# RWKV-7 and RetNet layer on one core: triangular blocks solved from the last row, the result transposed once

## The chip, the core and the metric

The kernel runs on one core of a Trainium2 chip. The engines of the core work side by side: TensorE (PE in the rows, its weight loads PEld) multiplies matrices, VectorE (DVE) works element by element, ScalarE (ACT) evaluates functions and copies, GpSimd (POOL) does a little of both, SyncE (SP) issues most of the DMAs. The metric is the device time of one execution in microseconds, as the median of several runs.

## What is computed

One decoder layer: 256 tokens, width 2048, float32. Half of the mixing width is RWKV-7 with 16 heads of 64, half is RetNet with 4 heads of 256; then an output projection, a norm, an MLP and a second norm.

```python
def _wkv7_scan(r, decay, k, v, a_vec, b_vec):
    def step(S, inp):
        r_t, w_t, k_t, v_t, a_t, b_t = inp
        sa = jnp.einsum('bhvk,bhk->bhv', S, a_t)
        S = (S * w_t[:, :, None, :] + sa[..., None] * b_t[:, :, None, :]
             + v_t[..., None] * k_t[:, :, None, :])
        y_t = jnp.einsum('bhvk,bhk->bhv', S, r_t)
        return S, y_t
...
def _hybrid_layer(x, ...):
    h = x @ w_in
    y_a = _rwkv7_mix(h[..., :RWKV_SHIFT_WIDTH], ...)
    q, k, v, g = jnp.split(h[..., RWKV_SHIFT_WIDTH:], RET_SPLITS, axis=-1)
    y_b = _retention_mix(q, k, v, g, ret_gn_w)
    mix = jnp.concatenate([y_a, y_b], axis=-1).astype(x.dtype) @ w_o
    x = _layer_norm(ALPHA * x + mix, ln1_w, ln1_b)
    ff = jnp.square(jax.nn.relu(x @ w_up)) @ w_down
    return _layer_norm(ALPHA * x + ff, ln2_w, ln2_b)
```

The recurrence over tokens is computed in chunks of 64. Within a chunk, what the state gains from earlier tokens of the same chunk is a triangular system: the inverse of a 64x64 triangular matrix for every head and chunk. That inverse is what the change touches.

## The kernel before

**Projections.** Every weight tile comes by DMA (`raw`, three buffers, L135), ScalarE casts it to a short float `whi` (L136), VectorE takes the rest `wlo` (L138), and TensorE multiplies three times for each product: `whi` with the high part of x, `whi` with the low part, `wlo` with the high part. `stat_tile` (L154) holds the weights and streams x through, 256 columns; `mov_chunk` (L170) does it the other way round, 512 columns. A weight tile has two halves, and a half is 24 matmuls of L154 or 12 of L170.

**Units.** The first 512 us hold four units u = 0 to 3 of four RWKV heads each (`rwkv_unit`), and retention's four heads between them. `large()` writes out the projections; `interleave` lets the units' generators take a step every so many projection steps (`LAG`). A unit waits in the text for a key of another with `until(...)`. The order of each engine's instructions is not the order of the text, though: a scheduler of the framework places them as its model holds them ready, so a small edit can move work far from it.

**One unit.** Decay: `s` (L542), a running sum `cs` over the 256 tokens of both head pairs as one scan of 512 elements (L544; the constant at `C_RS` is zero at the start of each chunk, which restarts the sum), exponentials `dc`, `di`, `s` on ScalarE (L548 to L550). Keys: `kkr` (L571), the square `sq`, and a head sum, that is `hi` on ScalarE (L558), `lo` on VectorE (L559) and two matmuls with a matrix of ones (L562, L563). The same head sum serves the bonus `bo` later in the unit. Then the Gram products `g1` (L623) and their mask (L625).

**The triangular blocks.** Each 64x64 triangle of `g1` is split in 32x32 blocks. The two on the diagonal are inverted by VectorE, the one off it by two matrix products `d1` (L726) and `d2` (L737). There are 16 triangles in a unit. `g1` goes to DRAM (`dn`), and from there into `blk`: 128 partitions, in four groups of 32, and each partition holds one block of 32x32 elements, row s behind row s − 1, every block four times with fewer rows each time (`diag`, L641). `xb` holds eight columns of the inverse for each partition and starts as pieces of the unit matrix (`eye`). The loop at L674 goes t = 1 to 31. Step t multiplies what is known of m = min(t, 8) pieces, t elements each, with column t of `blk` (`prod`, L677) and sums each piece into `xb` (L680). With t growing, fewer groups are at work: q = 128 partitions down to 32. The result goes by four DMAs to DRAM (`dxt`, L687) and by two into `xt` (L689). VectorE then turns the upper halves of it into `xx` (L715, two 32x256 transposes), `d1` multiplies `g1` with `xx`, ScalarE copies the product to `pt`, `d2` multiplies `pt` with `xt`, a copy puts that into `xt` (L742), and the scans of the chunks (L758 to L792) follow.

**Retention.** For each head VectorE multiplies q and k with the rotary table, `ra` (L417) and `rb` (L419), POOL turns them into `qk` (L422, L423), TensorE multiplies q with k (L434), VectorE multiplies with the mask `dmt` into `pm` (L439). `dmt` is loaded on POOL's queue.

**SBUF.** `LONG` names tiles with a buffer of their own; other names of `tmp` share `NSHORT` = 10 buffers.

Of the kernel before, what the change touches and what calls it, by code (L numbers as in the profile page):

```python
# [10 lines left out]
F32 = mybir.dt.float32  # L11
# [3 lines left out]
ALU = mybir.AluOpType  # L15
AX = mybir.AxisListType

P = 128
# [19 lines left out]
C_BO = C_RS + 512  # L38
# [3 lines left out]
def constants():  # L42
# [10 lines left out]
    rs = np.ones(512, np.float32)  # L53
    rs[::64] = 0.0
    c[:, C_RS:C_RS + 512] = rs
# [11 lines left out]
    eye = np.tile(np.eye(8, 32, dtype=np.float32).reshape(1, 256), (P, 1))  # L67
# [33 lines left out]
def tile_hybrid_layer(ctx, tc, xT, xtok, ws, pp, lup, glup, ln1r, ln2r, cst, rope, dmask, eye, out):  # L101
# [169 lines left out]
    with ExitStack() as rctx:  # L271
# [3 lines left out]
        LONG = ("k", "r", "v", "ar", "g1", "g2", "btok", "ktok", "vtok", "xt", "gg", "bg", "yc")  # L275
# [3 lines left out]
        def tmp(name, bufs=1, n=512):  # L279
            if name in LONG or n < 256:  # L280
                return rp.tile([P, n], F32, name=name, tag=name, bufs=2 if name in TWO else bufs)
            if name in RET:
                return rp.tile([P, n], F32, name=name, tag="rshort", bufs=4)
            return rp.tile([P, n], F32, name=name, tag="short", bufs=NSHORT)
# [11 lines left out]
        def diag(d, g, n):  # L296

            return bass.AP(tensor=d.tensor, offset=d.offset + 8 * 65 * g, ap=[[2080, 32], [64, n], [1, 32 - 8 * g]])
# [98 lines left out]
        def retention():  # L397

            for n in range(2):
# [9 lines left out]
                for h in (2 * n, 2 * n + 1):  # L409
# [21 lines left out]
                    dmt = rp.tile([P, T], F32, name="dmt", tag="dmt", bufs=2)  # L431
# [71 lines left out]
        def rwkv_unit(u):  # L503
# [4 lines left out]
            def until(*key):  # L508
                while key not in done:
                    yield 1  # L510
# [27 lines left out]
            for p, j in enumerate(js):  # L538
# [5 lines left out]
            V.tensor_tensor_scan(out=cs, data0=c1[:, C_RS:C_RS + 512], data1=s, initial=0.0,  # L544
                                 op0=ALU.mult, op1=ALU.add)
# [87 lines left out]

            g1v = g1.rearrange("q (g two x) -> q g two x", two=2, x=64)
# [4 lines left out]
            for g in range(4):  # L639
                m = 32 - 8 * g  # L640
                nc.sync.dma_start(out=blkv[32 * g:32 * g + 32, 0:m, 0:m], in_=diag(dn, g, m))  # L641
# [32 lines left out]
            for t in range(1, 32):  # L674
                q, m = 32 * ((39 - t) // 8), min(t, 8)
                pv = prod[0:q, 0:m * t].rearrange("q (j s) -> q j s", s=t)
                V.tensor_tensor(out=pv, in0=xbv[0:q, 0:m, 0:t],  # L677
                                in1=blk.rearrange("q (s t) -> q t s", t=32)[0:q, t:t + 1, 0:t].broadcast_to([q, m, t]),
                                op=ALU.mult)
                V.tensor_reduce(out=xbv[0:q, 0:m, t], in_=pv, axis=AX.X, op=ALU.add)  # L680
                if t in SUB_YIELD:
                    yield LAG["sub"]
            if u > 0:
                yield from until("end", u - 1)
            xt = tmp("xt")
            for g in range(4):
                nc.sync.dma_start(out=diag(dxt, g, 8), in_=xbv[32 * g:32 * g + 32, :, 0:32 - 8 * g])  # L687
            for h in range(2):
                nc.sync.dma_start(out=v8(xt)[64 * h:64 * h + 64], in_=rows(dxt, h))  # L689
# [5 lines left out]
            yield from until("v", u)  # L695
            v = done["v", u]
# [15 lines left out]
            xx = tmp("xx")[:, 0:256]  # L712
            for h in range(2):
                q = slice(64 * h, 64 * h + 32)
                V.transpose(out=xx[q].rearrange("q (g x) -> q g x", x=32), in_=v8(xt)[q, :, 0:32])  # L715
# [8 lines left out]
            def d1(r, p, n):  # L724
                o = 128 * (4 * p + n)
                TE.matmul(pb[r.start + 32:r.stop, c32(p, n)], g1[r.start:r.start + 32, o + 32:o + 64],  # L726
                          xx[r.start:r.start + 32, c32(p, n)], start=True, stop=True)
# [426 lines left out]
```

## Time and profile before

| what | value |
| --- | --- |
| median of 3 runs | 1284.11 us (1282.04 to 1285.03) |
| the profiled execution | 1282.36 us |
| its span | 1280.6 us |
| mean granted clock of TensorE | 0.991 |
| TensorE busy | 1233.7 us, 96% of the span |
| VectorE busy | 853.1 us, 67% |
| ScalarE busy | 560.0 us, 44% |
| GpSimd busy | 117.3 us, 9% |

The profiled execution lies among the runs; the rows below are of it, and its times are counted from the start of its span. The shares are averages over stages of a different kind: the units and retention up to about 512 us, then the output projection and the MLP.

### The profile page before, as it was taken

The numbers are of one execution on the slowest core, as the hardware profiler recorded it, in microseconds if no ns is written. First come the engines' busy times: TensorE is split into PE (matmuls) and PEld (weight loads), VectorE is DVE, ScalarE is ACT, GpSimd is POOL, SyncE is SP. The second block draws the span as 40 slices with busy tenths as digits, with TensorE's granted clock in tenths as the row PEclk, the third lists the DMA queues.
The fourth block names the chain that finished last, engine by engine and source line by source line (L and its number), as shares of the span: only waits on it lengthen the run. The fifth ranks groups of instructions, "written<-read, shape, count | busy, mean of one in ns | idle before, by whom it ended". The sixth has DMA issues, their size and how long they took to land.

```text
span 1280.6 us, 21924 instructions
## 1 busy us (share of the span) xinstructions
PE 1233.7 (96%) x8952; PEld 1110.1 (87%) x8952; DVE 853.1 (67%) x1311; ACT 560.0 (44%) x723; POOL 117.3 (9%) x97
## 2 busy tenths in 40 slices
PE   7998989999998999989999999999999999999996
PEld 7988888878897778769988899988999888999885
DVE  6898899899979765685654455545555554555566
ACT  5544335355434343464443344433444433444441
POOL 1100121110102100137300000000000000000001
PEclk9999999999999999999999999999999999999998
DMA  8565345345454437555655555555555555555562
GB/s 287 197 187 157 105 142 168 108 153 176 156 144 148 147 112 252 197 176 193 239 198 198 194 188 190 184 192 190 194 190 190 184 192 192 193 190 186 183 213 98
DMA packets 86185, 229.89 MB, mean 180 GB/s; under 512 B 30530, under 2 KB 30658, under 8 KB 85316
## 3 DMA queue, kind: packets, MB, share of 16 engines
q1 hardware_dynamic: 83924, 219.51, 52.5%
q0 software_dynamic: 1440, 7.87, 1.7%
q8 instruction: 70, 1.15, 0.4%
q10 hardware_dynamic: 720, 1.11, 0.3%
q14 instruction: 31, 0.25, 0.1%
HBM read 224.72 MB, written 3.74 MB: 178 GB/s over the span
## 4 chain that ended last, share of the span: by engine, by line
PE 75%; DVE 11%; ACT 3%; DMA 3%; issue 2%; POOL 1%; DVEq 0%; ACTq 0%; POOLq 0%; SPq 0%
PE mm L170 33%; PE mm L154 33%; PE mm L190 4%; DVE wlo L138 3%; DMA raw<-in_ws_dram 2%; DVE prod L677 2%; DVE xb L680 1%; PE sm L623 1%; ACT whi L136 1%; DMA xt<-dxt 1%; POOL qk L423 1%; ACT wx L136 0%; PE sm L766 0%; ACT sw L653 0%; PE sm L758 0%
## 5 line engine op out<-in xcount | busy, mean ns | idle before, releaser
L138 DVE TENSOR_TENSOR wlo<-raw,whi 128x1024 fp32r<-128x1024 f32 x375 | 466.6, 1245 | 330.4 <-ACT whi L136 319.6
L136 ACT CAST whi<-raw 128x1024 fp32r<-128x1024 f32 x376 | 395.0, 1051 | 548.5 <-PE mm L154 235.3
L154 PE MATMUL mm<-x1h,wlo 128*128 128x256 f32 x960 | 269.9, 281 | 0.0
L154 PE MATMUL mm<-x1l,whi 128*128 128x256 f32 x960 | 269.9, 281 | 0.0
L154 PE MATMUL mm<-x1h,whi 128*128 128x256 f32 x960 | 269.8, 281 | 0.0
L154 PEld LDWEIGHTS mm<-x1h,wlo 128*128 128x128 f32 x960 | 183.6, 191 | 0.0
L154 PE MATMUL mm<-xh,whi 128*128 128x256 f32 x640 | 181.8, 284 | 0.0
L154 PEld LDWEIGHTS mm<-x1h,whi 128*128 128x128 f32 x960 | 181.1, 189 | 0.1
L154 PEld LDWEIGHTS mm<-x1l,whi 128*128 128x128 f32 x960 | 180.2, 188 | 0.2
L154 PE MATMUL mm<-xl,whi 128*128 128x256 f32 x640 | 179.9, 281 | 0.0
L154 PE MATMUL mm<-xh,wlo 128*128 128x256 f32 x640 | 179.8, 281 | 0.0
L170 PE MATMUL mm<-whi,ul 128*128 128x512 f32 x448 | 174.3, 389 | 0.0
L170 PE MATMUL mm<-whi,uh 128*128 128x512 f32 x448 | 174.3, 389 | 0.0
L170 PE MATMUL mm<-wlo,uh 128*128 128x512 f32 x448 | 174.3, 389 | 0.0
L154 PEld LDWEIGHTS mm<-xh,whi 128*128 128x128 f32 x640 | 121.5, 190 | 2.9 <-issue 0.9
L154 PEld LDWEIGHTS mm<-xl,whi 128*128 128x128 f32 x640 | 121.5, 190 | 0.9 <-issue 0.2
L154 PEld LDWEIGHTS mm<-xh,wlo 128*128 128x128 f32 x640 | 121.6, 190 | 0.7
L170 PEld LDWEIGHTS mm<-whi,ul 128*128 128x128 f32 x448 | 84.1, 188 | 17.5
L170 PEld LDWEIGHTS mm<-whi,uh 128*128 128x128 f32 x448 | 84.1, 188 | 17.5
L170 PEld LDWEIGHTS mm<-wlo,uh 128*128 128x128 f32 x448 | 84.1, 188 | 17.1
L1044 POOL TENSOR_TENSOR z<-z,lnr 128x512 f32<-128x512 f32 x3 | 3.9, 1292 | 603.0 <-DVE stats L1032 603.0
L170 PE MATMUL mm<-whi,xh 128*128 128x512 f32 x128 | 51.7, 404 | 0.0
(270 smaller groups left out, 1612.5 us busy)
## 6 DMA issues: line engine op xcount, KB each, us to landing
raw<-in_ws_dram SPq DMA_DIRECT2D x400, 512.0 KB, 4.5
first<-in_ws_dram SPq DMA_DIRECT2D x8, 256.0 KB, 8.2
z<-in_xtok_dram POOLq DMA_DIRECT2D x2, 1024.0 KB, 10.8
lnr<-in_ln1r_dram POOLq DMA_DIRECT2D x2, 1024.0 KB, 5.5
lnr<-in_ln2r_dram POOLq DMA_DIRECT2D x2, 1024.0 KB, 11.2
xraw<-in_xT_dram SPq DMA_DIRECT2D x3, 512.0 KB, 8.8
dn<-g SPq DMA_DIRECT2D x8, 128.0 KB, 3.6
xt<-dxt SPq DMA_DIRECT2D x8, 128.0 KB, 3.6
```

The lines of the kernel that those rows point to most:

```text
L136: S.copy(hi, raw)
L138: E.tensor_tensor(out=lo, in0=raw, in1=hi.bitcast(F32), op=ALU.subtract)
L154: TE.matmul(dst, w[:, c], a, start=n == 0, stop=n == 3 * KT - 1)
L170: TE.matmul(dsts[tt], a, w[:, c], start=first and k4 == 0 and j == 0, stop=last and k4 == 3 and j == 2)
L190: TE.matmul(dst, a, wt[:, o:o + w], start=kq == 0 and k4 == 0 and i == 0, stop=kq == 3 and k4 == 3 and i == 2)
L423: G.tensor_tensor(out=o[:, hs[1]], in0=rb_[:, hs[0]], in1=rb_[:, hs[1]], op=ALU.add)
L623: TE.matmul(bank[r, 128 * n:128 * n + 128], src[r, c64(p, n)], ar[r, o:o + 128], start=True, stop=True)
L677: V.tensor_tensor(out=pv, in0=xbv[0:q, 0:m, 0:t], in1=blk.rearrange("q (s t) -> q t s", t=32)[0:q, t:t + 1, 0:t].broadcast_to([q, m, t]), ...
L680: V.tensor_reduce(out=xbv[0:q, 0:m, t], in_=pv, axis=AX.X, op=ALU.add)
L1044: G.tensor_tensor(out=z[:, tt, cb(n)], in0=z[:, tt, cb(n)], in1=lnr2[:, 0, cb(n)], op=ALU.mult)
```

## The change

The loop runs the same triangle from its last row. Step t takes s0 = 31 − t and multiplies the t known elements behind s0 with row s0 of `blk`, from s0 + 1 on. Where before the elements of that operand were 32 elements (128 bytes) apart, they now lie one behind the other. The pieces sit at the end of their rows, not at the start: `blk` is filled from 32 − m on, `xb` and `eye` are shifted by 24 or 8 − m places, and `diag` reads from another offset; the DMAs' shapes stay. What comes out is the inverse transposed, `xc`, a new tile with its own buffer. `d1` reads `xc` itself, so `xx` is gone; `xt` is made from `xc` by one 128x512 transpose before `d2`. The wait for the end of the unit before (`until("end", u - 1)`) stands behind the DMAs now, since `xc` and no longer `xt` is what they fill.

Room for `xc` comes from two places. `dmt` has one buffer, not two. The constant at `C_RS` has 256 columns, not 512, so its DMA is 128x640 and no longer 128x896, and the scan is two scans of 256.

```diff
--- before.py
+++ after.py
@@ -35,7 +35,7 @@
 C_ID = 0
 C_MG = 128
 C_RS = 256
-C_BO = C_RS + 512
+C_BO = C_RS + 256
 NC1 = C_BO + 128
 
 
@@ -50,9 +50,9 @@
         c[r, C_MG:C_MG + 64] = up
         c[r, C_MG + 64:C_MG + 128] = upi
         c[r, C_BO + 64 * h:C_BO + 64 * h + 64] = 1.0
-    rs = np.ones(512, np.float32)
+    rs = np.ones(256, np.float32)
     rs[::64] = 0.0
-    c[:, C_RS:C_RS + 512] = rs
+    c[:, C_RS:C_RS + 256] = rs
     pos = np.arange(T, dtype=np.float32)
     inv = (1.0 / (np.float32(10000.0) ** np.linspace(0.0, 1.0, 128, dtype=np.float32))).astype(np.float32)
     th = inv[:, None] * pos[None, :]
@@ -64,7 +64,7 @@
     dm = np.zeros((P, 4, 256), np.float32)
     for h in range(4):
         dm[:, h] = np.where(t >= m, np.exp((t - m) * lg[h]), 0.0) / 16.0
-    eye = np.tile(np.eye(8, 32, dtype=np.float32).reshape(1, 256), (P, 1))
+    eye = np.tile(np.eye(8, 32, 24, dtype=np.float32).reshape(1, 256), (P, 1))
     return c, rope, dm.reshape(P, 1024), eye
 
 
@@ -272,7 +272,7 @@
         rp = rctx.enter_context(tc.tile_pool(name="rp", bufs=1))
         dram = rctx.enter_context(tc.tile_pool(name="dram", bufs=1, space=bass.MemoryType.DRAM))
 
-        LONG = ("k", "r", "v", "ar", "g1", "g2", "btok", "ktok", "vtok", "xt", "gg", "bg", "yc")
+        LONG = ("k", "r", "v", "ar", "g1", "g2", "btok", "ktok", "vtok", "xt", "xc", "gg", "bg", "yc")
         TWO = ("ar", "g1", "g2", "btok", "ktok", "dtot")
         RET = ("ra", "rb", "qk0", "qk1", "pm", "gth", "tm")
 
@@ -293,9 +293,9 @@
 
             return bass.AP(tensor=d.tensor, offset=d.offset + 8 * 4160 * h, ap=[[64, 64], [4160, 8], [1, 64]])
 
-        def diag(d, g, n):
-
-            return bass.AP(tensor=d.tensor, offset=d.offset + 8 * 65 * g, ap=[[2080, 32], [64, n], [1, 32 - 8 * g]])
+        def diag(d, m, n):
+
+            return bass.AP(tensor=d.tensor, offset=d.offset + 64 * (m - n), ap=[[2080, 32], [64, n], [1, m]])
 
 
         first = [([rp.tile([P, 1024], F32, name="first", tag=t, bufs=n) for t, n in tags],
@@ -428,7 +428,7 @@
                     yield
                     yield
                     sc = sm_bank()
-                    dmt = rp.tile([P, T], F32, name="dmt", tag="dmt", bufs=2)
+                    dmt = rp.tile([P, T], F32, name="dmt", tag="dmt", bufs=1)
                     nc.gpsimd.dma_start(out=dmt, in_=dmask[:, T * h:T * h + T])
                     for i in range(2):
                         TE.matmul(sc[:, 0:T], k[:, T * i:T * i + P], q[:, hs[i]], start=i == 0, stop=i == 1)
@@ -541,8 +541,9 @@
             yield LAG["scan"]
             V.tensor_scalar(out=s, in0=s, scalar1=0.5, scalar2=0.5, op0=ALU.mult, op1=ALU.add)
             cs = tmp("cs")
-            V.tensor_tensor_scan(out=cs, data0=c1[:, C_RS:C_RS + 512], data1=s, initial=0.0,
-                                 op0=ALU.mult, op1=ALU.add)
+            for h in hs:
+                V.tensor_tensor_scan(out=cs[:, h], data0=c1[:, C_RS:C_RS + 256], data1=s[:, h], initial=0.0,
+                                     op0=ALU.mult, op1=ALU.add)
             V.tensor_tensor(out=s, in0=cs, in1=s, op=ALU.subtract)
             dc, di = tmp("dc"), tmp("di")
             S.activation(dc, cs, AF.Exp, scale=-DECAY)
@@ -631,6 +632,7 @@
 
 
 
+
             g1v = g1.rearrange("q (g two x) -> q g two x", two=2, x=64)
             for h in range(2):
                 nc.sync.dma_start(out=rows(dn, h), in_=g1v[64 * h:64 * h + 64, :, 0, :])
@@ -638,7 +640,7 @@
             blkv = blk.rearrange("q (s t) -> q s t", t=32)
             for g in range(4):
                 m = 32 - 8 * g
-                nc.sync.dma_start(out=blkv[32 * g:32 * g + 32, 0:m, 0:m], in_=diag(dn, g, m))
+                nc.sync.dma_start(out=blkv[32 * g:32 * g + 32, 32 - m:32, 32 - m:32], in_=diag(dn, m, m))
 
             def tok(src, name):
 
@@ -672,27 +674,28 @@
             prod = rp.tile([P, 256], F32, name="prod", tag="prod", bufs=1)
             xbv = xb.rearrange("q (j t) -> q j t", t=32)
             for t in range(1, 32):
-                q, m = 32 * ((39 - t) // 8), min(t, 8)
+                q, m, s0 = 32 * ((39 - t) // 8), min(t, 8), 31 - t
                 pv = prod[0:q, 0:m * t].rearrange("q (j s) -> q j s", s=t)
-                V.tensor_tensor(out=pv, in0=xbv[0:q, 0:m, 0:t],
-                                in1=blk.rearrange("q (s t) -> q t s", t=32)[0:q, t:t + 1, 0:t].broadcast_to([q, m, t]),
-                                op=ALU.mult)
-                V.tensor_reduce(out=xbv[0:q, 0:m, t], in_=pv, axis=AX.X, op=ALU.add)
+                V.tensor_tensor(out=pv, in0=xbv[0:q, 8 - m:8, s0 + 1:32],
+                                in1=blkv[0:q, s0:s0 + 1, s0 + 1:32].broadcast_to([q, m, t]), op=ALU.mult)
+                V.tensor_reduce(out=xbv[0:q, 8 - m:8, s0], in_=pv, axis=AX.X, op=ALU.add)
                 if t in SUB_YIELD:
                     yield LAG["sub"]
-            if u > 0:
-                yield from until("end", u - 1)
-            xt = tmp("xt")
+
+            xc = tmp("xc")
             for g in range(4):
-                nc.sync.dma_start(out=diag(dxt, g, 8), in_=xbv[32 * g:32 * g + 32, :, 0:32 - 8 * g])
+                m = 32 - 8 * g
+                nc.sync.dma_start(out=diag(dxt, m, 8), in_=xbv[32 * g:32 * g + 32, :, 32 - m:32])
             for h in range(2):
-                nc.sync.dma_start(out=v8(xt)[64 * h:64 * h + 64], in_=rows(dxt, h))
+                nc.sync.dma_start(out=v8(xc)[64 * h:64 * h + 64], in_=rows(dxt, h))
             glupt = rp.tile([P, T], F32, name="glupt", tag="glupt", bufs=1)
             nc.gpsimd.dma_start(out=glupt, in_=glup[:, cu])
             done["front", u] = True
 
 
             yield from until("v", u)
+            if u > 0:
+                yield from until("end", u - 1)
             v = done["v", u]
             vtok = tok(v, "vtok")
             glus = split(glupt)
@@ -709,10 +712,8 @@
                 V.scalar_tensor_tensor(out=bg[:, hs[p]], in0=bg[:, hs[p]], scalar=pcol(GNB, j), in1=g[:, hs[p]],
                                        op0=ALU.add, op1=ALU.mult)
             done["free", "v", u] = True
-            xx = tmp("xx")[:, 0:256]
-            for h in range(2):
-                q = slice(64 * h, 64 * h + 32)
-                V.transpose(out=xx[q].rearrange("q (g x) -> q g x", x=32), in_=v8(xt)[q, :, 0:32])
+            xt = tmp("xt")
+            V.transpose(out=xt, in_=xc)
             yield LAG["bg"]
 
 
@@ -722,9 +723,9 @@
             pb, pt = sm_bank(), tmp("pt")[:, 0:256]
 
             def d1(r, p, n):
-                o = 128 * (4 * p + n)
-                TE.matmul(pb[r.start + 32:r.stop, c32(p, n)], g1[r.start:r.start + 32, o + 32:o + 64],
-                          xx[r.start:r.start + 32, c32(p, n)], start=True, stop=True)
+                o = 64 * (4 * p + n)
+                TE.matmul(pb[r.start + 32:r.stop, c32(p, n)], g1[r.start:r.start + 32, 2 * o + 32:2 * o + 64],
+                          xc[r.start:r.start + 32, o:o + 32], start=True, stop=True)
             each(d1)
             for h in range(2):
                 S.copy(pt[64 * h + 32:64 * h + 64], pb[64 * h + 32:64 * h + 64, 0:256])
```

The first place is VectorE at the end of unit 0's substitution; `prod` and `xb` are its products and sums, `wlo` a weight tile's low part, `r` and `ar` work of units 0 and 1, `xx` the transposes before `d1`, `kkr` the scaled keys of unit 1. Before:

```order
166 L240 SCALAR_TENSOR_TENSOR r<-mm,ppt,r 128x255
167 L677 TENSOR_TENSOR prod<-xb,blk 32x248
168 L680 TENSOR_REDUCE xb<-prod 32x8
169 L138 TENSOR_TENSOR wlo<-raw,whi 128x1024
170 L240 SCALAR_TENSOR_TENSOR r<-mm,ppt,r 128x255
171 L610 TENSOR_TENSOR ar<-r,dc 128x8x64
172 L138 TENSOR_TENSOR wlo<-raw,whi 128x1024 x2
173 L715 STREAM_TRANSPOSE xx<-xt 32x256
174 L571 TENSOR_SCALAR kkr<-k,dp 128x256 x2
175 L715 STREAM_TRANSPOSE xx<-xt 32x256
```

After, further ahead in the same substitution:

```order
155 L572 TENSOR_SCALAR kkr<-k,dp 128x256
156 L679 TENSOR_TENSOR prod<-xb,blk 32x208
157 L138 TENSOR_TENSOR wlo<-raw,whi 128x1024
158 L681 TENSOR_REDUCE xb<-prod 32x8
159 L560 TENSOR_TENSOR lo<-sq,hi 128x512
160 L679 TENSOR_TENSOR prod<-xb,blk 32x216
161 L138 TENSOR_TENSOR wlo<-raw,whi 128x1024
162 L681 TENSOR_REDUCE xb<-prod 32x8
```

The scaled keys `kkr` and the `lo` of their square's head sum now stand among the products, before the last sum; before, they stood behind it.

The second place is TensorE at `d1` of unit 1 (L726 before, L727 after); `mm` are the banks of the projections, `hi` and `lo` with `ones` the head sum of the squared keys. Before:

```order
1480 L726 MATMUL sm<-xx,g_1674 32x32
1481 L154 MATMUL mm<-xl,whi 128x256
1482 L154 MATMUL mm<-xh,wlo 128x256
1483 L154 MATMUL mm<-xh,whi 128x256
1484 L154 MATMUL mm<-xl,whi 128x256
1485 L154 MATMUL mm<-xh,wlo 128x256
1486 L154 MATMUL mm<-xh,whi 128x256
1487 L154 MATMUL mm<-xl,whi 128x256
1488 L726 MATMUL sm<-xx,g_1674 32x32 x15
```

After:

```order
1441 L727 MATMUL sm<-xc,g_1675 32x32
1442 L563 MATMUL sm<-hi,ones 128x512
1443 L564 MATMUL sm<-lo,ones 128x512
1444 L154 MATMUL mm<-xl,whi 128x256
1445 L154 MATMUL mm<-xh,wlo 128x256
1446 L154 MATMUL mm<-xh,whi 128x256
```

The first of the sixteen products stands 39 projection matmuls earlier, and the head sum, before at 1500 and 1504, right behind it. Counted in projection matmuls of L154 from the start, unit 0's `d1` stands 14 later than before, the q·k product L434 behind it 10 later, and the head sum of unit 1's bonus 21 later. In units 2 and 3 TensorE's order is as before. ScalarE and SP change by single places.

## Rows read from the trace of the kernel before

**Rows 1.** Stretches: length, each engine's busy time (instructions), granted clock, DMA share, GB/s.

```profile
96.00:128.00 32.00, 27.85 (x225) 27.05 (x224) 28.73 (x54) 15.90 (x25) 2.94 (x3) 0.95 0.51 156
...
160.00:192.00 32.00, 28.79 (x229) 27.88 (x230) 29.32 (x94) 12.29 (x17) 7.36 (x7) 0.95 0.44 143
...
384.00:416.00 32.00, 27.13 (x210) 25.62 (x208) 31.34 (x77) 15.84 (x24) 6.47 (x5) 1.00 0.45 148
640.00:960.00 320.00, 320.00 (x2009) 290.07 (x2008) 167.49 (x158) 136.33 (x144) 0.00 (x0) 1.00 0.58 192
```

**Rows 2.** TensorE's waits, 0 to 520 us: total, times, longest.

```profile
PE sm L562 <- ACT hi L558: 5.3, 4, 2.4
PE sm L434 <- POOL qk L423: 4.8, 4, 2.0
PE sm L434 <- POOL qk L422: 4.5, 3, 2.5
PE sm L726 <- DVE xx L715: 2.4, 2, 1.5
```

**Rows 3.** VectorE by shape, 0 to 520 us: busy us, mean ns, idle before.

```profile
L138 DVE TENSOR_TENSOR wlo<-raw,whi 128x1024 fp32r<-128x1024 f32 x136 | 165.7, 1220 | 42.8 <-ACT whi L136 39.8 <-PE mm L170 1.6 <-ACT mxh L482 1.2
...
L544 DVE TENSOR_TENSOR_SCAN cs<-c,s 128x512 f32<-128x512 f32 x4 | 4.9, 1219 | 0.1
...
L715 DVE STREAM_TRANSPOSE xx<-xt 32x256 f32<-32x256 f32 x8 | 3.5, 432 | 2.1 <-DMA xt<-dxt 1.9
...
L559 DVE TENSOR_TENSOR lo<-sq,hi 128x512 fp32r<-128x512 f32 x4 | 2.8, 693 | 0.0
...
L571 DVE TENSOR_SCALAR kkr<-k,dp 128x256 f32<-128x256 f32 x8 | 2.5, 336 | 0.1
...
L677 DVE TENSOR_TENSOR prod<-xb,blk 32x248 f32<-32x248 f32 x4 | 2.4, 607 | 0.1
...
L680 DVE TENSOR_REDUCE xb<-prod 32x8 f32<-32x248 f32 x4 | 1.6, 400 | 0.1
```

**Rows 4.** Stretch 0 to 520 us, line L677 alone: VectorE busy.

```profile
0.00:520.00 520.00, 48.35 (x124) 0.99 0.52 166
```

**Rows 5.** The same stretch, line L680 alone.

```profile
0.00:520.00 520.00, 34.01 (x124) 0.99 0.52 166
```

**Rows 6.** Chain of waits around unit 0: start us, us, what.

```profile
102.55 6.97 PE mm L154 x47
...
119.82 0.41 DVE xb L680
120.25 2.51 DMA dxt<-xb
...
122.83 3.90 DMA xt<-dxt
...
127.24 0.24 PE sm L726 x2
```

**Rows 7.** The same chain in unit 1.

```profile
204.33 16.12 PE mm L154 x139
```

**Rows 8.** The same chain in unit 3.

```profile
392.53 0.34 DVE pm L439
...
414.66 0.60 DVE ra L417
...
416.74 2.12 POOL qk L423
```

**Rows 9.** Stretches at the lower clock, columns as in rows 1.

```profile
102.50:106.00 3.50, 3.50 (x19) 3.50 (x18) 3.50 (x10) 0.89 (x2) 2.40 (x2) 0.51 0.46 154
...
201.60:205.00 3.40, 3.17 (x13) 2.98 (x14) 3.40 (x7) 3.11 (x5) 0.56 (x1) 0.50 0.17 51
...
416.60:420.00 3.40, 3.12 (x8) 1.97 (x8) 1.97 (x4) 0.00 (x0) 2.11 (x1) 0.50 0.20 73
```

**Rows 10.** POOL in order of time, 385 to 440 us, idle before in brackets.

```profile
402.16 0.98 POOL L422 TENSOR_TENSOR qk<-ra 128x256 f32<-128x256 f32 x1 [11.78 <-DVE rsq_h L259]
```

## The prediction

> **What bounds the kernel now.** I read the stretches first. From 640 to 960 us TensorE is busy 320.00 of 320 us and VectorE 167.49: that later part can only start sooner, not get shorter. The change touches the first 512 us, the four RWKV units, so a gain must be time in which TensorE stands still or runs at its lower level there. In 96 to 128, 160 to 192 and 384 to 416 TensorE is busy 27 to 29 of 32 us, and VectorE 28.7 to 31.3 [rows 1]: here VectorE is full. Second, TensorE's waits [rows 2]: 9.3 us for the turned q and k of retention (POOL's two lines, fed by VectorE's `ra` and `rb`), 5.3 us for the cast `hi` of the head sums, 2.4 us for `xx` before the product `d1` (1.5 in unit 0, so 0.9 in unit 1; units 2 and 3 do not wait). That is 17 us, and it is all that a faster VectorE can give, with what the clock loses behind such waits: the granted clock falls to 0.50 or 0.51 (1.2 of 2.4 GHz) in 102.5 to 106, 201.6 to 205 and 416.6 to 420 [rows 9], each time behind one of the waits for `hi` or `qk` (the longest 2.4 and 2.5 us [rows 2]), and a fourth time near 174 behind another of them. Behind the first, 47 projection matmuls take 6.97 us [rows 6]; at the 16.12 us of 139 [rows 7], 0.116 each, they would take 5.45. So one fall costs 1.5 us among projections.
>
> **The products, the centre of the change.** A unit has 31 products of m*t elements, 3884 elements together. Before, the operand from `blk` is a column, with 128 bytes from one element to the next; after, it is a piece of a row. The largest product takes 607 ns, the sum over the same 248 elements 400 [rows 3], and that sum reads its elements one behind the other. The excess is 207 ns, or 0.83 ns an element. If it is the price of the column, a unit saves 3884 x 0.83 = 3.2 us. The bounds: the 124 products take 48.35 us and the 124 sums 34.01 [rows 4, 5], so at the sums' price 14.3 us fall away, 3.6 a unit; and if the stride costs nothing, 0. I take 3.2, nearest to the one pair of rows that differs in this alone as far as I can see. [...]
>
> **What else VectorE gains and pays.** The scan is split in two. By the 1219 ns of the whole [rows 3], half plus a start is some 0.65 to 0.7, so +0.1 us a unit. The two `xx` transposes go (2 x 0.432 [rows 3]) and one 128x512 comes, by their 256 elements and its 512 an estimate of 0.7; so −0.2 us, and it stands before `d2`, no longer before `d1`: some 0.5 us come off the way to `d1`. What hides the new transpose is projection work between `d1` and `d2`; without it, it would cost 0.7 a unit. The shorter constant (128x640 in place of 128x896) and the moved pieces of the DMAs, which keep their shapes, cost nothing: no engine waits for the first, and the chain from the last sum over `dxt` and `xc` keeps its 2.51 + 3.90 us [rows 6]. With one `dmt` the load of the next head's mask waits on POOL's queue for the multiply `pm` of the head before; for the last head that multiply is at 392.53 [rows 8] and POOL's next work behind the load at 402.16, after 11.78 us without any [rows 10]: nothing, and without that cover the turning of q would start later by as much as `pm` is behind it. The moved wait for the end of the unit before (`until`) lets the DMAs of `dxt` go out earlier in the text; SP's queue holds the raw weight loads beside them, and the order there differs by a place or two; I count 0, with 0.5 us either way.
>
> **Where the saving reaches TensorE.** The order moves work too, in units 0 and 1; in units 2 and 3 TensorE's order is the same.
>
> Unit 0: the last sum ends at 120.2, and `d1` starts at 127.24 after a wait of 1.5 [rows 2, 6]. VectorE saves 3.2 in products, but two `kkr` (2 x 0.336), one `lo` (0.693) and one more `wlo` (1.22 [rows 3]) now stand ahead of the last sum: 2.6 us. So `xc` lands 0.6 earlier and, with no `xx`, `d1` can start 1.1 earlier. TensorE has 14 more projection matmuls ahead of it, 14 x 0.116 = 1.6 us: the wait of 1.5 is covered. −1.5.
>
> The turned heads near 170 us: 3.3 of the 9.3 us of waits [rows 2] are here. The products there have under 65 elements and save 0.1; ten more matmuls, 1.2 us, stand ahead, and `ra` comes some 0.5 later in VectorE's order. −0.7, the clock still falls.
>
> Unit 1: the head sum waits 2.4 us for `hi`. Its cast comes some 1.3 later in the new order, but 21 more matmuls (2.4 us) stand ahead: −1.1. `d1` stands 39 matmuls (4.5 us) earlier; VectorE has 3.2 less of products and three `wlo` less (3.7) ahead of the last sum, and 1.4 more of `kkr` and `lo`, 0.5 less for `xx`: 6.0 earlier against 4.5 + 1.1, so the wait stays what it is, about 0.9. With what I may have missed of the queue ahead (0 to +1), −1.0.
>
> Unit 2: VectorE has room, −0.3.
>
> Unit 3: VectorE is busy 31.34 of 32 us [rows 1]. `ra` of the last head starts at 414.66 and POOL's `qk` after `rb` at 416.74 [rows 8]. Products ahead of it since 390, t = 20 to 29, have 1960 elements: 1960 x 0.83 = 1.6 us, and two more stand between `ra` and `rb`, 0.3 in all to gain. The bound is the wait itself, 2.5 [rows 2]; what is late next is the projection that fills the bank. I take −1.8, and −0.5 for the head before, whose `ra` also stands behind products. The wait then falls from 2.5 to about 0.7, and the clock need not fall: those 3.4 us at the lower level hold eight matmuls [rows 9], so at full speed I count half of a fall among projections, −0.7.
>
> Sum: −1.5 − 0.7 − 1.0 − 0.3 − 0.5 − 1.8 − 0.7 = −6.5 us of the 14 that VectorE is relieved of. The profiled execution took 1282.36 (span 1280.6), the median of the runs 1284.11, 1.75 more: −6.5 gives 1275.9 by the one and 1277.6 by the other. I take the middle of the two bases, 1283.2 (1283.24), and so **forecast 1276.8**, its own range 1273.5 to 1279.5.
>
> **Rivals.** (1) *Only the last unit's chain pays.* In units 0 and 1 waits move from place to place. For: three of the four stretches have a queue of `wlo`, `kkr` and `lo` behind the products, which fills the room. Then −0.5 − 1.8 − 0.7 = −3.0: 1280.2. (2) *The clock stays up as well.* If the shortened waits near 101, 174 and 201 no longer let it fall, three times 1.5 come on top: −11.0, 1272.2. Against: the wait at 101 hangs on the scan of the unit behind, ahead of which the products are short. (3) *The other side: the column was free.* Two operands, of which one repeats, cost 607 ns in any layout. [...] The reordering then stands alone. In unit 0 the 2.6 us of moved work come ahead of the last sum, against 1.6 of cover and 0.5 of `xx`: +0.5. In unit 1 `d1` is 4.5 us earlier for TensorE, `xc` only 2.8: +1.7, a wait of 2.6, and the clock falls behind both waits, +3.0; less 1.1 at the head sum and 0.7 near 170. With the scan's halves (0.4) that is +3.8: 1287. It decides when a unit saves under some 1.2 us, a third of what I take. Against: the rows of the sums. (4) *Part of the price stays*, some 0.3 ns an element are saved, and gain and order cancel: about 1283, no change.
>
> **Chances.** Forecast 0.53, (1) 0.15, (2) 0.12, (3) 0.10, (4) 0.10. A measurement of this kernel tells about 0.2%, 2.6 us, from no change: faster is under 1281.5. Forecast, (2) and two thirds of (1) are faster: 0.75; (4) and the rest of (1) the same: 0.15; (3) slower, 0.10. The range goes from 1271.0, with half of (2) below it, to 1283.5, with (3) and half of (4) above.
>
> **What would show it.** Products of 248 elements at about 400 ns, 124 of them at 34 to 37 us; `d1` of unit 0 without a wait; POOL's last `qk` two us sooner, and no fall of the clock near 417. Wrong it would be if the products kept 500 ns or more, if a wait over 2 us stood before `d1` of unit 1, or if the waits for `hi` grew by as much as the others fell.

## The result, and the profile after

| kernel | median of its runs | executions | ratio to before, 95% interval |
| --- | --- | --- | --- |
| before | 1285.03 us (1280.24 to 1296.06) | 11 | |
| changed | 1274.39 us (1270.25 to 1279.05) | 11 | 0.991 (0.9887 to 0.9932) |

The changed kernel is faster by 0.9%, some 11 us; the forecast was 1276.8, within 1271.0 to 1283.5. The profiled execution of the changed kernel took 1279.05 us (span 1277.3) and was the slowest of its eleven, while the one of before, 1282.36, was among the faster ones. The difference of the two profiles, 3.3 us, is therefore no measure of the change, and further profiles of both kernels stand below. The ratios of this document leave out executions more than 1.5% above the fastest of the same kernel (one of ten with columns, two of six in the third measurement of the changed kernel, one of four with the longer lag behind the bonus).

VectorE by shape in the changed kernel, 0 to 520 us (columns as in rows 3; L545 is the scan, L716 the single transpose, L679 the product, L681 the sum):

```profile
L545 DVE TENSOR_TENSOR_SCAN cs<-c,s 128x256 f32<-128x256 f32 x8 | 5.2, 677 | 0.1
...
L716 DVE STREAM_TRANSPOSE xt<-xc 128x512 f32<-128x512 f32 x4 | 2.8, 701 | 0.0
...
L679 DVE TENSOR_TENSOR prod<-xb,blk 32x248 f32<-32x248 f32 x4 | 1.6, 400 | 0.1
L681 DVE TENSOR_REDUCE xb<-prod 32x8 f32<-32x248 f32 x4 | 1.6, 396 | 0.1
```

The product takes what the sum over the same elements takes, 400 and 396 ns; before, it was 607 [rows 3]. Line L679 alone over 0 to 520 us, for [rows 4]:

```profile
0.00:520.00 520.00, 35.60 (x124) 0.97 0.52 165
```

That is 12.75 us less for the same 124 products. TensorE's waits in the same stretch (L727 is `d1`, L563 the head sum's first matmul), for [rows 2]:

```profile
PE sm L727 <- DMA xc<-dxt: 4.9, 2, 3.1
PE sm L434 <- POOL qk L423: 4.9, 4, 1.9
PE sm L434 <- POOL qk L422: 2.9, 3, 1.3
PE sm L563 <- ACT hi L559: 1.8, 2, 1.0
```

The four rows of before hold 17.0 us and these 14.5. The waits for `hi` shrank from 5.3 to 1.8 and those for `qk` from 9.3 to 7.8, while the wait before `d1` doubled from 2.4 to 4.9, and what ends it is now the DMA itself, not `xx`. The stretches, for [rows 1]:

```profile
96.00:128.00 32.00, 27.96 (x237) 27.06 (x237) 26.26 (x53) 16.40 (x24) 6.55 (x7) 1.00 0.57 182
128.00:160.00 32.00, 32.00 (x377) 28.28 (x377) 18.95 (x40) 7.36 (x15) 1.26 (x1) 0.68 0.13 40
160.00:192.00 32.00, 29.03 (x268) 27.91 (x269) 30.69 (x90) 12.75 (x20) 6.81 (x6) 1.00 0.54 158
384.00:416.00 32.00, 29.82 (x235) 28.82 (x234) 29.80 (x82) 15.87 (x24) 6.25 (x5) 0.95 0.48 155
```

Beside [rows 1] TensorE is busy 0.1 to 0.2 us longer in 96 to 128 and 160 to 192, whose clock is at 1.00 where it was 0.95. The 2.7 us more in 384 to 416 are mostly not a gain: the last head's wait for `qk`, 2.46 us up to 416.35 before, lies behind 416 here, 1.34 us up to 418.60 (over 384 to 448 the busy time is 58.5 us before and 59.5 after). In that stretch the clock is now at 0.95. And 128 to 160, in the profile of before

```profile
128.00:160.00 32.00, 32.00 (x473) 28.46 (x471) 26.69 (x53) 11.76 (x22) 4.63 (x6) 1.00 0.37 105
```

has a granted clock of 0.68 in place of 1.00, with TensorE busy throughout in both. The chain of waits around `d1` of unit 0, for [rows 6]:

```profile
119.24 3.67 DMA dxt<-xb
...
122.93 4.26 DMA xc<-dxt
...
127.23 0.24 PE sm L727 x2
```

The last sum ends 1.0 us earlier than before, the two DMAs take 7.9 us instead of 6.4, and `d1` starts at the same time as before, with 14 more projection matmuls done ahead of it.

### The profile page after: what moved, and what is told of

Read it like the earlier page. It is cut to its first block, busy times and chain, and to the rows that moved or that the text cites. A ratio compares the mean times of both kernels' runs of the same rounds, so it can differ in the third digit from the quotient of the medians.

```text
span 1277.3 us, 21921 instructions
## 1 busy us (share of the span) xinstructions
PE 1235.4 (97%) x8952; PEld 1113.0 (87%) x8952; DVE 841.8 (66%) x1311; ACT 560.6 (44%) x723; POOL 120.0 (9%) x97
## 4 chain that ended last, share of the span: by engine, by line
PE 79%; DVE 9%; DMA 6%; ACT 2%; issue 2%; POOL 1%; SPq 0%; DVEq 0%; ACTq 0%; POOLq 0%
PE mm L154 37%; PE mm L170 31%; DMA raw<-in_ws_dram 4%; PE mm L190 4%; DVE wlo L138 3%; PE sm L624 1%; PE mm L381 1%; DVE prod L679 1%; DVE xb L681 1%; DMA xc<-dxt 1%; ACT whi L136 1%; DMA first<-in_ws_dram 1%; POOL qk L423 1%; PE sm L759 1%; PE sm L767 0%
## 5 line engine op out<-in xcount | busy, mean ns | idle before, releaser
L154 PE MATMUL mm<-x1h,wlo 128*128 128x256 f32 x960 | 268.9, 280 | 0.0
L154 PE MATMUL mm<-x1h,whi 128*128 128x256 f32 x960 | 268.8, 280 | 0.0
L154 PE MATMUL mm<-x1l,whi 128*128 128x256 f32 x960 | 268.8, 280 | 0.0
L154 PE MATMUL mm<-xh,whi 128*128 128x256 f32 x640 | 183.6, 287 | 0.0
L154 PEld LDWEIGHTS mm<-x1h,wlo 128*128 128x128 f32 x960 | 183.5, 191 | 0.0
L154 PE MATMUL mm<-xl,whi 128*128 128x256 f32 x640 | 181.4, 283 | 0.0
L154 PE MATMUL mm<-xh,wlo 128*128 128x256 f32 x640 | 180.6, 282 | 0.0
L154 PEld LDWEIGHTS mm<-x1l,whi 128*128 128x128 f32 x960 | 180.2, 188 | 0.2
L154 PEld LDWEIGHTS mm<-x1h,whi 128*128 128x128 f32 x960 | 180.2, 188 | 0.1
L154 PEld LDWEIGHTS mm<-xh,whi 128*128 128x128 f32 x640 | 122.7, 192 | 3.5 <-issue 1.2
L154 PEld LDWEIGHTS mm<-xl,whi 128*128 128x128 f32 x640 | 122.5, 191 | 1.0
L154 PEld LDWEIGHTS mm<-xh,wlo 128*128 128x128 f32 x640 | 122.8, 192 | 0.6
L170 PEld LDWEIGHTS mm<-wlo,uh 128*128 128x128 f32 x448 | 84.1, 188 | 17.1
```

Source lines behind the costliest of these rows:

```text
L154: TE.matmul(dst, w[:, c], a, start=n == 0, stop=n == 3 * KT - 1)
L170: TE.matmul(dsts[tt], a, w[:, c], start=first and k4 == 0 and j == 0, stop=last and k4 == 3 and j == 2)
```

## The experiments

**The price of the column.** Two kernels differ from the two measured ones in the second operand of the product alone; the order of the instructions on every engine stays. In one, the changed kernel reads a column again (it multiplies other elements of the block than the solution needs):

```diff
-in1=blkv[0:q, s0:s0 + 1, s0 + 1:32].broadcast_to([q, m, t]), op=ALU.mult)
+in1=blk.rearrange("q (s t) -> q t s", t=32)[0:q, s0:s0 + 1, s0 + 1:32].broadcast_to([q, m, t]), op=ALU.mult)
```

> The changed kernel, but each product reads a column of blk again (128 bytes from one element to the next); every engine's order is as in the changed kernel, the values multiplied are others. Theory (the column is the price): the 124 products take 47 to 49 us again, not 35.6, and the time goes back to the kernel before or over it, 1284 to 1290, since the moved work stays. Rival (new order, d1 straight from xc and the single transpose make the gain): products may cost 48 us, but the time stays within 2 us of the changed kernel, 1272 to 1277.

In the other, the kernel before reads a row (again other elements), and nothing else of the change is done:

```diff
-in1=blk.rearrange("q (s t) -> q t s", t=32)[0:q, t:t + 1, 0:t].broadcast_to([q, m, t]),
+in1=blkv[0:q, t:t + 1, 0:t].broadcast_to([q, m, t]),
```

> The kernel before, but each product reads a row of blk; every engine's order is as in the kernel before, the values multiplied are others. Theory: products take 35 to 37 us, and most of the gain is here without any other part of the change: 1274 to 1279, ratio 0.991 to 0.996; the waits for qk of the last head and for hi shrink, the wait before d1 of unit 0 stays near 1 us. Rival (order and layout make the gain): 1282 to 1286, ratio 0.998 to 1.002.

Line L679 of the first, then L677 of the second, 0 to 520 us, VectorE busy:

```profile
0.00:520.00 520.00, 48.45 (x124) 0.97 0.51 162
```

```profile
0.00:520.00 520.00, 35.72 (x124) 0.97 0.52 165
```

The first came out at a ratio to before of 1.0013 (0.9985 to 1.0041), the second at 0.991 (0.988 to 0.994), the same as the whole change. So, within these intervals, the row is the whole gain, and all else in the change (the transposed result, `d1` straight from `xc`, the split scan, one mask buffer, the moved work) is worth nothing that can be told from 0: +0.13%, between −0.15 and +0.41%. TensorE's waits show the same. (The wait before `d1` of unit 0 was to stay near 1 us in the second; it was 2.3.) Those of before with rows:

```profile
PE sm L434 <- POOL qk L423: 5.3, 4, 1.9
PE sm L726 <- DVE xx L715: 3.3, 2, 2.3
PE sm L562 <- ACT hi L558: 2.8, 2, 1.6
PE sm L434 <- POOL qk L422: 2.8, 3, 1.4
```

and those of the changed kernel with columns:

```profile
PE sm L727 <- DMA xc<-dxt: 5.9, 2, 3.4
PE sm L434 <- POOL qk L423: 5.3, 4, 1.9
PE sm L434 <- POOL qk L422: 4.4, 3, 2.2
PE sm L563 <- ACT hi L559: 2.6, 2, 1.4
```

Their sums are 14.2 and 18.2 us, against 17.0 and 14.5 for the kernels that they come from. The order of the changed kernel alone adds to the wait before `d1` (5.9 in place of 2.4), as the third rival had it. The time shows no loss, but its interval, up to +0.41% or 5.3 us, does not exclude that rival's 3.8 us either. The moved `until` does not enter at all: with it put back to its old place, the order of every engine is the same, so that was not run.

**What makes a column dear.** The kernel before, with the second operand from the constant tile at another distance in each unit (other values, and the products no longer wait for `blk`):

```diff
-q, m = 32 * ((39 - t) // 8), min(t, 8)
+q, m, step = 32 * ((39 - t) // 8), min(t, 8), (2, 3, 4, 16)[u]
...
-in1=blk.rearrange("q (s t) -> q t s", t=32)[0:q, t:t + 1, 0:t].broadcast_to([q, m, t]),
+in1=c1.rearrange("q (o x) -> q o x", o=1)[0:q, :, 0:t * step:step].broadcast_to([q, m, t]),
```

> The kernel before, but each product reads its second operand from the constant tile, with 2, 3, 4 and 16 elements (8, 12, 16 and 64 bytes) from one element to the next in units 0, 1, 2 and 3; the values are others, and the products no longer wait for blk, so its time is not compared, only the products' durations. Theory (the price is a new piece of memory for each element): 32x248 takes 400 ns at 8 bytes, between 400 and 607 at 12, 607 at 16 and at 64, as at 128. Rival (the price grows with the distance): 400 to 430 up to 16 bytes and more at 64. Second rival (any stride but one costs): about 607 at all four.

The largest product of each unit in VectorE's order of time (start, us, shapes), with 8, 12, 16 and 64 bytes from one element to the next:

```profile
92.48 0.40 DVE L677 TENSOR_TENSOR prod<-xb,c 32x248 f32<-32x248 f32 x1
```

```profile
167.87 0.48 DVE L677 TENSOR_TENSOR prod<-xb,c 32x248 f32<-32x248 f32 x1
```

```profile
254.47 0.61 DVE L677 TENSOR_TENSOR prod<-xb,c 32x248 f32<-32x248 f32 x1
```

```profile
311.98 0.56 DVE L677 TENSOR_TENSOR prod<-xb,c 32x248 f32<-32x248 f32 x1
```

0.40, 0.48, 0.61 and 0.56 us, beside 0.40 at 4 bytes and 0.607 at 128 [rows 3]. In these runs the price begins above 8 bytes, is complete at 16, and does not grow from there to 64 and 128. Nor is the 0.56 a fall with the distance: the product of unit 3 is the shortest of the four at 128 bytes too, 0.58 us in the profile of before, where the others take 0.61 to 0.62.

**The clock behind d1.** The changed kernel was profiled twice more.

> The changed kernel once more, for a second profile. Theory: the long stretch at the lower clock behind d1 of unit 0 (128 to 149 us, 0.51 granted) is not in every execution; a fast execution (span near 1270) has no such stretch, or one of some 3.5 us, and the wait before d1 is 1 to 3 us. Rival: the stretch belongs to the new order, then it is here again, about 20 us long, and the spread of the runs has another cause. Ratio to the kernel before 0.991 by both.

> The changed kernel, as the yardstick of the same call: ratio to the kernel before 0.989 to 0.993; a third profile, in which the stretch at the lower clock behind d1 of unit 0 is seen again (0.5 over 10 to 21 us) if it belongs to this order at this place.

The ratios to before were 0.9898 (0.9869 to 0.9926) and 0.9899 (0.9853 to 0.9945). The stretch 128 to 160 us of the two (columns as in rows 1):

```profile
128.00:160.00 32.00, 32.00 (x376) 28.34 (x374) 18.66 (x40) 7.37 (x15) 1.27 (x1) 0.68 0.14 45
```

```profile
128.00:160.00 32.00, 32.00 (x470) 28.90 (x470) 27.37 (x53) 9.89 (x19) 3.68 (x3) 0.97 0.29 74
```

The same program, the same place: 0.68 with 376 matmuls in the one, as in the first profile, and 0.97 with 470 in the other. The second profile alone spoke for the rival: the stretch was there again, 20.5 us long as in the first. The third refutes it: the long stretch at the lower level does not belong to the order, it comes in some executions. It could still follow from the length of the wait before `d1` (3.1, 2.9 and 2.6 us in the three), and kernels with that place moved were to show it.

The lag of the squared keys' head sum from 5 to 6 steps:

> The changed kernel with the lag of the squared keys' head sum raised from 5 to 6 steps; on TensorE d1 of unit 0 then stands about 25 projection matmuls (2.9 us) later, d1 of unit 1 some 100 later, and that head sum no longer right behind d1. Theory (TensorE comes too early to d1, and the long stretch at the lower clock follows that wait): the wait before d1 of unit 0 falls from 3 us to under 1, the clock in 128 to 160 us is 0.95 or more instead of 0.68, and the time is 5 to 10 us under the changed kernel, 1264 to 1270. Rival (the landing of xc moves with it, or the clock falls for another reason there): a wait over 2 us, or a clock of 0.7 to 0.85 in that stretch without one, and a time within 3 us of the changed kernel's.

The stretch, and the waits in 120 to 135 us:

```profile
128.00:160.00 32.00, 31.14 (x460) 28.16 (x461) 25.10 (x49) 8.84 (x18) 2.39 (x2) 0.95 0.30 83
```

```profile
PE sm L727 <- DMA xc<-dxt: 4.1, 1, 4.1
```

The wait before `d1` of unit 0 did not go, it grew to 4.1 us, since the landing moved with it, and behind this longest wait of all the clock stood at 0.95. The time, 0.9928 (0.9899 to 0.9956), is that of the changed kernel. What decides whether the clock comes back at once, the runs don't show.

**A later d1.** The lag between the steps of the keys' root from 1 to 2, in the changed kernel twice and in the kernel before once:

> The changed kernel with the lag between the steps of the keys' root raised from 1 to 2; d1 of unit 0 then stands two halves of a weight tile (48 projection matmuls, 5.6 us) later on TensorE, d1 of unit 1 over four halves later, the head sum still right behind d1. Theory: no wait before either d1, clock 0.95 or more in 128 to 160, and the time 5 to 10 us under the changed kernel, if the later scans of the units stay covered. Rival: same time within 3 us, the waits before qk and hi growing by what d1 gives back.

> The changed kernel with the lag of 2 between the root's steps once more, beside the changed kernel on the same chip. If its gain is real: ratio to the kernel before 0.985 to 0.989 and at least 0.2% under the changed kernel's; if the four executions of the first time were lucky: 0.990 to 0.993, the same as the changed kernel's.

> The kernel before with the lag of 2 between the root's steps and nothing else. Theory (the later d1 pays because the faster products let TensorE arrive too early there, and before there was 1.5 us of wait to win): ratio to the kernel before 0.997 to 1.001. Rival (the lag is a gain of its own, unrelated to the change): 0.992 to 0.996, as much as it brings on the changed kernel.

In 120 to 135 us the wait before `d1` is 1.6 and 1.8 us in the two executions of the changed kernel, and 128 to 160 us reads:

```profile
128.00:160.00 32.00, 30.44 (x462) 27.18 (x461) 25.00 (x50) 9.07 (x19) 3.96 (x3) 1.00 0.32 81
```

```profile
128.00:160.00 32.00, 30.21 (x332) 25.91 (x332) 15.43 (x33) 7.38 (x15) 3.07 (x2) 0.68 0.25 74
```

The first time the ratio to before was 0.9873 (0.9825 to 0.9921), the second time 0.9904 (0.9865 to 0.9942), beside 0.9899 for the changed kernel measured with it: no gain that holds. Behind the wait of 1.8 us the clock stood at 0.68. The first expectation of that lag, no wait before `d1`, was a miss too. In the kernel before, the same lag costs 0.9% (1.0087, 1.0055 to 1.0119). TensorE's longest row of waits there:

```profile
PE sm L726 <- DVE xx L715: 10.3, 4, 4.9
```

Four waits before `d1`, up to 4.9 us: with products that are dear, the moved work seems to leave VectorE still later. That is a reading; no run takes it apart. Nor did a longer lag behind the bonus settle anything:

> The changed kernel with the lag behind the bonus raised from 4 to 6 steps; on TensorE d1 of unit 1 then stands 1.8 halves of a weight tile (about 5 us of projections) later, d1 of unit 0 where it was. Theory (the wait before d1 of unit 1 comes from d1 standing ahead of the landing of xc): that wait, 1.8 us in the profile, is gone, and the time is 1.5 to 3 us under the changed kernel. Rival (the landing is late because other loads share the DMA engines, and follows): a wait over 1 us stays before it, and the time is the same.

`d1` of unit 1 waited 2.3 us although it stood five us later, so the rival's sign came: the landing follows. That other loads share the DMA engines is its reason, and not shown; what the rows show is that the first of the two DMAs took 5.5 us, where it takes 1.5 in the changed kernel. The ratio on record, 0.9833 (0.9787 to 0.988), is of three executions from 1262.88 to 1279.01 us, the fourth took 1285.41: too few and too far apart for a verdict on the time.

**The kernel before, a second profile.**

> The kernel before once more, for a second profile. If the first profile is typical: waits for hi near 5.3 us and for qk near 9.3, the clock at 0.95 in the same four stretches, 8 us of products' price as before, and the work behind the units (from the end of the fourth unit's last projections on) 835 us long against 830 to 832 in the changed kernel's profiles. If that last difference is chance, it is 830 to 833 here too.

It took 1285.98 us, span 1284.2. Its waits, in the columns of rows 2, and its stretch from 128 to 160:

```profile
PE sm L434 <- POOL qk L422: 4.8, 3, 2.8
PE sm L434 <- POOL qk L423: 4.8, 4, 2.0
PE sm L562 <- ACT hi L558: 4.2, 2, 2.3
PE sm L726 <- DVE xx L715: 2.8, 1, 2.8
```

```profile
128.00:160.00 32.00, 30.85 (x418) 27.31 (x419) 23.19 (x48) 9.62 (x19) 3.47 (x4) 0.89 0.26 85
```

The sum, 16.6 us, is near the 17.0 of the first profile. But `d1` of unit 0 waits 2.8 us here, not 1.5, and the clock behind it is at 0.89, not 1.00. The first profile had shown a fortunate execution of that place. The last head's first q·k product has the same TensorE work ahead of it in both kernels, so it is a mark to compare them by. TensorE in order of time, in the two profiles of before and the three of the changed kernel:

```profile
416.35 0.99 PE L434 MATMUL sm<-qk,qk 128*128 128x256 f32 x2 [2.46 <-POOL qk L422]
```

```profile
422.48 1.01 PE L434 MATMUL sm<-qk,qk 128*128 128x256 f32 x2 [2.80 <-POOL qk L422]
```

```profile
418.60 0.70 PE L434 MATMUL sm<-qk,qk 128*128 128x256 f32 x2 [1.34 <-POOL qk L422]
```

```profile
417.24 0.70 PE L434 MATMUL sm<-qk,qk 128*128 128x256 f32 x2 [1.39 <-POOL qk L422]
```

```profile
414.97 0.70 PE L434 MATMUL sm<-qk,qk 128*128 128x256 f32 x2 [1.35 <-POOL qk L422]
```

The means are 419.4 and 416.9: 2.5 us are gained by then. The sums of waits differ by as much (16.8 against 14.4, with 14.1 and 14.6 in the two further profiles), but that is an accident, since two things stand against each other here. TensorE from the start to the mark, in the first profile of each kernel (columns as in rows 1):

```profile
0.00:416.35 416.35, 387.97 (x3561) 355.31 (x3561) 360.36 (x764) 194.27 (x303) 52.60 (x58) 0.99 0.52 164
```

```profile
0.00:418.60 418.60, 393.68 (x3561) 361.57 (x3562) 348.58 (x765) 194.39 (x303) 53.54 (x58) 0.97 0.52 162
```

The mark less the busy time is all the time that TensorE stood still: 28.4 us in both profiles of before, and 24.9, 23.9 and 24.5 us in the three after, so 4.0 us less. But the profiles of the changed kernel ran longer at the lower clock on their way to the mark: 0.97, 0.97 and 0.98 granted, beside 0.99 and 0.98 before.

From the mark to the end of the span there are 864.3 and 861.7 us before, and 858.7, 858.4 and 859.3 after: another 4.2 us. Three places hold them.

- From the mark to unit 3's first scan product (L758, in the changed kernel L759) it is 26.6 us in both profiles of before and 26.0 in the three after: 0.7 us, the rest of that head's wait and the fall of the clock near 417, which is gone (1.00 in 415 to 423).
- From the first norm's first transpose (L914, L915) to the MLP's first matmul of L154 it is 24.6 and 24.7 us before and 22.4 to 22.5 after: 2.2 us. VectorE and POOL work there side by side, each on the low part `wx` of a weight tile, in the first profile of before and the second of after:

```profile
544.13 3.41 DVE L138 TENSOR_TENSOR wx<-raw,wx 128x1024 fp32r<-128x1024 f32 x1
544.08 2.38 POOL L138 TENSOR_TENSOR wx<-raw,wx 128x1024 fp32r<-128x1024 f32 x1 [0.16 <-ACT wx L136]
```

```profile
543.76 1.21 DVE L138 TENSOR_TENSOR wx<-raw,wx 128x1024 fp32r<-128x1024 f32 x1
543.92 3.31 POOL L138 TENSOR_TENSOR wx<-raw,wx 128x1024 fp32r<-128x1024 f32 x1 [0.37 <-ACT wx L136]
```

  The one that starts first keeps its 1.2 or 2.4 us here, the other takes 3.3 or 3.4; where that is VectorE, TensorE waits some 2.2 us longer. The two start 0.04 to 0.4 us apart. The price of the products does not decide it: the second execution with the lag of 2 and the one with the longer lag behind the bonus read rows and have 24.7 us, the kernel before with the lag of 2 reads columns and has 22.5.
- From that matmul to the end it is 712.2 and 709.7 us before and 709.7 to 709.8 after: the first profile of before is 2.5 us longer, 1.2 in the mean. The kernel before with rows has the same 2.5 us more, the changed kernel with columns has not; the cause is open.

So some 3.4 of the 4.2 us go with the execution that was profiled and not with the change. The expectation's own measure agrees: from TensorE's transposes in L473 on, just behind the last projections of the units' stage, the first profile of before has 835.2 us, the second 832.7, the three of after 830.4, 830.0 and 831.0. By its words the difference was chance.

## Why the prediction was right

- **The products.** Forecast 3.2 us a unit, measured 12.75 / 4 = 3.2. The choice between the ends, by the one pair of rows that differed in nothing else, was the step that carried the forecast, and the two kernels that change that operand alone show that it carries the whole result.
- **Scan and transposes.** Two scans of 677 ns for one of 1219, +0.13 us; one transpose of 701 ns for two of 432, −0.16. Both as put down, and both without trace in the time.
- **Unit 0.** The net, −1.5, is what the rows give (`d1` at 127.23 with 14 matmuls, 1.6 us, more done), but the way was another. The forecast left TensorE's arrival at `d1` as it was and the two DMAs at 6.4 us. In fact the head sum near 100 us waited 0.8 us instead of 2.3 and the clock did not fall behind it (102.5 to 106: 1.00 in place of 0.51), which the forecast had only as a part of its second rival; and some 3 us of that went back before `d1`, since the DMAs took 7.9 us. The failing step is "keeps its 2.51 + 3.90 us"; why they took longer, the runs don't show. That two misses cancelled, and the net came out, is luck. Of the sign "`d1` of unit 0 without a wait" the profiles show the opposite: 3.1, 2.9 and 2.6 us.
- **Near 170 and unit 1.** The `qk` waits near 170 fell from 3.2 to 3.0, where a fall by 0.7 was forecast, but the clock stayed up (in the third profile it fell there again). Unit 1's head sum gained 1.4 (forecast 1.1), its `d1` waited 1.8 instead of the 0.9 that were to stay, and 0.9 and 2.0 in the further profiles.
- **The last heads.** Forecast −2.3. The last two heads wait for the first half of `qk` (L422) 3.2 us before, for the second (L423) 2.2; after it is 1.7 and 2.9:

```profile
PE sm L434 <- POOL qk L423: 2.9, 2, 1.9
PE sm L434 <- POOL qk L422: 1.7, 2, 1.3
```

  that is −0.8. In the last head the wait for the first half fell from 2.5 to 1.3, that for the second grew from 0.3 to 1.0. The forecast took a projection for what is late next; POOL's second half, 2.12 us from 416.74 on [rows 8], was. That the clock would not fall near 417 was right, but in all three profiles it falls one head earlier, between 389 and 398, where it did not in the first profile of before (in the second it did). POOL's last `qk`, forecast two us sooner, ended near 421.0, 419.6 and 417.4 us, beside 418.9 and 425.0 before.
- **The size.** −6.5 was forecast, about −11 measured (0.991 of 1285.03; by the interval −8.7 to −14.5). The waits were sized too large: the terms without the clock add up to −5.8, while the four rows of waits gave 2.4 us and all of TensorE's standing still up to the mark 4.0. The term sized too small is the clock, −0.7. In the two further measurements of the changed kernel, each beside executions of before, the mean span is 10.5 and 11.6 us shorter; (1 − granted clock) × span, an estimate of what the lower level takes, falls from 17.9 to 13.4 and from 17.1 to 11.8 us. So about 5 of the 11 us go with the clock, which rival (2) had at −4.5 on top of the forecast. With the 4 us of standing still, some 2 us remain that no row places. The base, 1283.2, was 1.8 us under the median of the eleven, which brought the forecast time nearer to the measured one by luck: from 1285.03, −6.5 is 1278.5.
- **The rivals.** The free column is refuted by both kernels. Its second half, that the moved work alone makes waits before `d1`, shows in the rows (5.9 us); its time, 0.13% or 1.7 us in the middle of the interval, is under the 3.8 us put down, which the interval still holds. That only the last unit pays is refuted by the size, since the interval of the gain begins at 8.7 us; that waits move from place to place, its reason, is what the rows show (`hi` −3.5, `d1` +2.5). That the clock stays up as well, −11.0 and 1272.2, has the measured size and was half right in its places: in the first profile the clock stays up at all four, but new falls stand behind `d1` of both units and near 396 us.

## What to carry to other kernels

In these runs a product of VectorE with one float32 operand read at 16, 64 or 128 bytes from one element to the next took 0.56 to 0.62 us for 248 elements, and 0.39 to 0.41 at 4 and 8 bytes. In another kernel, compare such an instruction's time with that of another one on the same number of elements, and turn the algorithm around (here, from the last row on) or the layout, so that the elements lie one behind the other. Try the access alone first, with other values if need be: it told here in one run what of a large change was the gain. A wait that one engine no longer causes can go to what is late next: the one before `d1`, 2.4 us for VectorE's `xx` in the first profile of before, is 4.9 us for the landing of `xc` in the first of after.

## What the runs showed of the hardware

- The price of distance: 0.40, 0.48, 0.61 and 0.56 us for 248 elements at 8, 12, 16 and 64 bytes, and 0.40 at 4. All of it comes between 8 and 16 bytes; from 16 to 64 nothing is added.
- After a wait of 3.1 us TensorE's granted clock stayed at 0.51 for 21 us although it was busy all the time (128 to 149 us), in the third profile of the same program, after 2.6 us, for some 3.4. Behind 4.1 us of wait, in the kernel with the head sum's lag at 6, it came back as soon (0.95 over 128 to 160), behind 1.8 us, in the second execution with the root's lag at 2, it did not (0.68). In the first profile of the changed kernel the 256-column matmuls of L154 start 0.213 us apart near 135 us, at 0.50, and 0.113 near 640 us, at 1.00; no run gives the clock in GHz, as the forecast puts it beside its 0.50 and 0.51. The eleven executions of the changed kernel go with their mean granted clock: spans of 1277.3 us at 0.985, 1272.7 at 0.989, 1268.5 at 0.991. A single profile of such a kernel shows one draw of it.
- The way over DRAM and back, two small DMAs behind each other, took 6.4 us in the first profile of before and 7.9 in the first of after, with the same shapes and one weight load between them in both; it was 7.3 in the second profile of before, 6.6 in the changed kernel with columns and 7.5 in the kernel before with rows.
- VectorE and POOL on a `wx` of 128x1024 at the same time: the one that started first took 2.38 us (POOL, first profile of before) or 1.21 us (VectorE, second of after), the other 3.41 and 3.31.
